# Two AdaLN steps per pass of the first branch, input sums in other attention units, border loads and stores reordered, in a one-core decoder layer

## The chip, the cores and the metric

The kernel runs on one core of one Trainium2 chip. The metric is device time in microseconds (us), the median of several executions. Beside the times there is one profiled execution, recorded by the hardware profiler; rows of it have the start in us from the beginning of its span, the duration, the engine, the line of the kernel and the operation. Five engines work side by side, each in the order of its own instruction stream: TensorE (PE, with PEld for its weight loads), VectorE (DVE), ScalarE (ACT), GpSimd (POOL) and SyncE (SP), which here only issues DMA transfers. ScalarE and GpSimd can issue transfers too.

## The reference

One decoder layer in float32, 1024 tokens, width 1024. AdaLN turns a condition vector into six vectors of 1024, which scale, shift and gate the two halves of the layer:

```python
c_act = jax.nn.silu(c)
mod = (jnp.einsum('bd,de->be', c_act, w_ada[l]) + b_ada[l])[:, None, :]
shift_m, scale_m, gate_m, shift_f, scale_f, gate_f = jnp.split(mod, 6, axis=-1)
u = x * (1.0 + scale_m) + shift_m
y = mixer(u, positions, w_in[l], sinks[l], w_branch_a[l], w_branch_b[l], w_o[l])
x = layer_norm(DEEPNORM_ALPHA * x + (1.0 + gate_m) * y, ln1_g[l], ln1_b[l])
u = x * (1.0 + scale_f) + shift_f
y = swiglu(u, w_gate_up[l], w_down[l])
x = layer_norm(DEEPNORM_ALPHA * x + (1.0 + gate_f) * y, ln2_g[l], ln2_b[l])
```

The mixer has two attentions beside each other. A is a sliding window with 16 query heads and a sink term. B is dilated attention, 24 heads in three patterns of 8, whose three outputs are combined by a softmax over their log-sum-exp. Each goes through its own output matrix, the two results are weighted with sigmoid gates computed from u, added, and multiplied by `w_o`.

## The kernel before

Every product is made from float32 numbers split in two parts, high and low, each of a type (F32R) that TensorE multiplies in one pass: a product is hi·hi + hi·lo + lo·hi, three matmuls. ScalarE makes the high part, VectorE subtracts to get the low part (`split`; L78 and L79 for the weights of the `Weights` streams, L144 and L145 for those of the `Pairs` streams). The `gate` products of the mixer and the gate_up products are made by a seven-product scheme on halves, whose operands are differences of halves of u; these are called t1 to t4 here ("t sums").

The stages, in order. First projections (from the first us on), then 20 **attention units** (12 of B, 8 of A), each in four parts `i` = 0 to 3. While one unit's scores, probabilities and outputs are computed, a generator (`stream`, moved on by `pump`) runs the projections and rotations of the next units between them: a q projection ends in TensorE's tile `pj`, VectorE multiplies it by the cosine (L548, L549), POOL by the sine and adds (L551, L552), ScalarE and VectorE split the result into `qs` (L565, L566), and TensorE multiplies `kh` and `qs` to scores (L624). `tasks(n, i)` is called once in each part and puts in small work for earlier units: sending statistics, `combine_apply` (L774 and L777, merging B's three patterns), the stores of finished A outputs (`scale_a`), and `input_sums`, which makes the t sums. One call chain of `input_sums` handles a row block k and a column half c in four parts: load x into the tile `cst`, scale and shift by ScalarE (L881), four subtractions by VectorE (L883 to L886), store to `t_d`. Before the change units with n%3==1 take one (k, c) and units with n%3==2 the next, for the first twelve units.

At the end of the attention, the **border** to the next stage: the last A outputs go to DRAM (`oa_d`, `wa_d`) from SyncE's queue, SyncE loads the weight pairs of the first gates (`gw.load`), and the t sums, tile by tile (`load_sum`, L1046), into four buffers `xs`; ScalarE (L1019) and VectorE (L1020) split them. Then the **gate products** (L1030): 42 products of 12 matmuls.

In the gate stage begins `ada_steps` (L978), a generator for the AdaLN vectors m = 2 to 5. For each m it loads eight row blocks of `w_ada` (512 KB, tile `a_raw`, two buffers), and adds each, times its entry of c, into `acc` on VectorE (L987 the first, L989 the others); each `next` issues one load and one sum, of the block before. After the eight sums there is one empty step, and then the sum over partitions: for m = 2 and 5 two float32 matmuls against `ones` (L998) and an addition of the bias, for m = 3 and 4 eight narrow matmuls (L1005). Fourteen `next` calls lie in the gate stage.

Then the **branch stage**: 24 passes (`steps`), eight output blocks `dc` each for three operand sets b = 0, 1, 2. A pass makes two products of four blocks from a weight stream (`ws.take`, `ws.step`) and the split attention outputs `parts` (`o_part`, which loads `o_raw` from `oa_d` and `ob_d`), merges them into `merged` (ScalarE for b = 0, VectorE and POOL for b = 1, 2), and calls `next(ada)` once. In the last branch `split_merged` splits a finished row block for the final product, two passes behind; blocks 6 and 7 follow after the loop, and then what is left of `ada_steps`. Then W_o's products, a first layer norm, gate_up, down, and a second layer norm.

The order of work on each engine is the order in which the Python code emits it; a framework adds the waits between engines and for buffers. DMA transfers from one engine's queue are issued in that order, and a transfer that waits holds up those behind it in its queue.

Of the kernel before, what the change touches and what calls it, by code (L numbers as in the profile page):

```python
# [10 lines left out]
F32 = mybir.dt.float32  # L11
F32R = mybir.dt.float32r
# [6 lines left out]
P = 128  # L19
T = 1024  # L20
# [129 lines left out]
def decoder_layer(ctx: ExitStack, tc: tile.TileContext, I, out, dbg=None):  # L150
# [565 lines left out]
    def send_sums(p):  # L716
        es = sums.pop(("es", p))
        pt = ps_t.tile([P, 4, P], F32, name="pt")
        nc.tensor.transpose(pt[:16, 0, :], es.rearrange("p h b -> p (h b)"), ident)
        sr = att.tile([32, P], F32, name="sr", bufs=2)  # L720
        nc.vector.tensor_copy(sr[:16], pt[:16, 0, :])
        nc.sync.dma_start(wa_d[p].rearrange("h (b q) -> (h b) q", q=P), sr[:16])

    def fetch_bcast(key, src):
        last = key in [(B_PAIRS - 1, g) for g in range(3)]
# [5 lines left out]
    def scale_a(p):  # L731
        o = outs.pop(p)
        nc.vector.tensor_tensor(o, o, sums.pop(p), op=OP.mult)
        nc.sync.dma_start(oa_d[p], o)
        if "oa" in dbg:
            nc.sync.dma_start(dbg["oa"][p], o)

# [103 lines left out]
    def tasks(n, i):  # L841

        last = unit(n - 1)
        if "b" in last and i == 0:
            send_stats(last)
            if last["b"][1] == 2:
                combine_load(last["b"][0])
        parts = (combine_shares, combine_weights, lambda p: fetch_bcast((p, 0), wt_d[p, 0]))
        if "b" in last and last["b"][1] == 2 and i > (last["b"][0] == B_PAIRS - 1):
            parts[i - 1 - (last["b"][0] == B_PAIRS - 1)](last["b"][0])  # L850
        if "a" in last and i == 2:
            send_sums(last["a"])
        if "a" in last and i == 3 and last["a"] < A_PAIRS - 1:
            fetch_bcast(last["a"], wa_d[last["a"]])
        last = unit(n - 2)
        if last.get("b", (0, 0))[1] == 2:
            p = last["b"][0]
            if i:
                combine_apply(p, i - 1)
            if (p < B_PAIRS - 1) <= i < 3:  # L860
                fetch_bcast((p, i), wt_d[p, i])
        if "a" in last and i == 1 and last["a"] < A_PAIRS - 1:
            scale_a(last["a"])
        if n % 3 and n < 12:
            input_sums(*divmod(2 * (n // 3) + n % 3 - 1, 2), i)

    def input_sums(k, c, i):

        cols = slice(c * 256, (c + 1) * 256)
        if i == 0:  # L870
            sums["x"] = buf = att.tile([P, T], F32, name="cst", bufs=1)
            for h in range(2):
                nc.sync.dma_start(buf[:, h * TH:(h + 1) * TH].rearrange("p (t c) -> p t c", t=2),
                                  I["xT"][k + 4 * h].rearrange("p (t c) -> p t c", t=2)[:, :, cols])
            return
        buf = sums["x"]
        r11, r12, r21, r22 = [buf[:, x * 256:(x + 1) * 256] for x in range(4)]
        if i == 1:
            for h in range(2):
                part, mod = buf[:, h * TH:(h + 1) * TH], mods[k + 4 * h]  # L880
                nc.scalar.activation(part, part, AF.Identity, bias=mod[:, 0:1], scale=mod[:, 1:2])  # L881
        elif i == 2:
            nc.vector.tensor_tensor(r11, r12, r11, op=OP.subtract)  # L883
            nc.vector.tensor_tensor(r12, r22, r12, op=OP.subtract)
            nc.vector.tensor_tensor(r22, r22, r11, op=OP.subtract)
            nc.vector.tensor_tensor(r21, r21, r22, op=OP.subtract)  # L886
        else:
            nc.sync.dma_start(t_d[:, k, :, cols].rearrange("s p c -> p s c"), buf.rearrange("p (s c) -> p s c", s=4))
# [11 lines left out]
    for s in range(len(subs) + 2):  # L900
        n, i = divmod(s, 4)
        start = ends[min(n, len(units) - 1)] + LEAD if n < len(units) else total
        stop = ends[n + 1] + LEAD if n + 1 < len(units) else total
        at = lambda x: pump(min(int(start + (stop - start) * (i + x) / 4), total - 1))
        if s < len(subs):
            un, qr = subs[s]
            if qr == 0:
                un["st"] = att.tile([P, 2, 2, NB], F32, name="st", bufs=3)
            scores(un, qr)
        at(0.4)  # L910
        if 1 <= s <= len(subs):
            turn_probs(*subs[s - 1])
        if s < len(subs):
            exponentials(*subs[s])
        at(0.8)
        if s >= 2:
            un, qr = subs[s - 2]
            if qr % 2:
                weigh(un, qr // 2)
                if qr == 3:  # L920
                    outs[un["a"] if "a" in un else un["b"]] = un["o"]
                    if "a" in un:
                        keep_sums(un)
                        if un["a"] == A_PAIRS - 1:
                            nc.sync.dma_start(oa_d[un["a"]], un["o"])
        tasks(n, i)
        at(1.0)
    pump(total)
# [46 lines left out]

    shsc = misc.tile([P, 2, KC], F32, name="shsc")

    def ada_steps():  # L978
        for m in (2, 3, 4, 5):
            acc = mix.tile([P, T], F32, name="acc", bufs=1)  # L980
            raws = {}
            for k in range(KC + 1):
                if k < KC:
                    raws[k] = mix.tile([P, T], F32, name="a_raw", bufs=2)
                    nc.sync.dma_start(raws[k], I["w_ada"][k * P:(k + 1) * P, m * D:(m + 1) * D])
                if k == 1:
                    nc.vector.tensor_scalar(acc, raws[0], c_act[:, 0:1], None, op0=OP.mult)  # L987
                elif k > 1:
                    nc.vector.scalar_tensor_tensor(acc, raws[k - 1], c_act[:, k - 1:k], acc, op0=OP.mult, op1=OP.add)  # L989
                yield  # L990
            yield
            if m in (2, 5):
                gt = (mix if m == 2 else misc).tile([P, T], F32, name=f"gate{m}", bufs=1)
                nc.sync.dma_start(gt, I["b_ada"][:, m * D:(m + 1) * D].to_broadcast([P, D]))
                for t in range(2):
                    s = slice(t * TH, (t + 1) * TH)
                    ps = ps_2.tile([P, TH], F32, name="p2")
                    nc.tensor.matmul(ps, ones, acc[:, s], start=True, stop=True)  # L998
                    nc.vector.tensor_tensor(gt[:, s], ps, gt[:, s], op=OP.add)
                nc.vector.tensor_scalar(gt, gt, 1.0, None, op0=OP.add)  # L1000
                gates[m] = gt
            else:
                ps = ps_2.tile([P, TH], F32, name="p2")
                for k in range(KC):
                    nc.tensor.matmul(ps[:, k:k + 1], acc[:, k * P:(k + 1) * P], ones[:, :1], start=True, stop=True)  # L1005
                nc.vector.tensor_tensor(shsc[:, m - 3], ps[:, :KC], b_pp[:, m * 8:m * 8 + 8], op=OP.add)
                if m == 4:
                    nc.vector.tensor_scalar(shsc[:, 1], shsc[:, 1], 1.0, None, op0=OP.add)
# [29 lines left out]
    operand("t4", bigu)  # L1038

    T_AT = {"t1": 0, "t3": 1, "t4": 2, "t2": 3}  # L1040
    t_todo = [(name, k) for name in ("t2", "t1", "t3", "t4") for k in range(4)]
    t_raw = {}

    def load_sum(name, k):
        t_raw[name, k] = gp.tile([P, TH], F32, name="xs", bufs=4)
        nc.sync.dma_start(t_raw[name, k], t_d[T_AT[name], k])  # L1046

    def next_sums(n):
        for _ in range(n):
            if t_todo:  # L1050
                name, k = t_todo.pop(0)
                split_to(name, k, t_raw.pop((name, k)))
                if len(t_todo) > 3:
                    load_sum(*t_todo[3])

    def piece():
        ws.step()
        gw.ready.append(ws.done[ws.used][:2])
        ws.used += 1

    gw.load(0)
    for x in t_todo[:4]:
        load_sum(*x)
    gw.load(1)
    for step in range(4):
        gw.add(0, step)
    acc, gated = {}, {}
# [34 lines left out]
    for n in range(2 * EARLY_PAIRS):  # L1102
# [3 lines left out]
        while len(gw.ready) < min(3, 2 * EARLY_PAIRS - 1 - n):  # L1106
            piece()
        prepare(n + 4 - 2 * EARLY_PAIRS)
        next_sums(2)
        after()  # L1110
        if n in (4, 6, 7):
            early_gate((4, 6, 7).index(n))
# [29 lines left out]
    for p in range(len(gate_pairs)):  # L1142
        ps = dict(zip("ab", acc[p])) if p in acc else {}
        g, last = {}, p == len(gate_pairs) - 1
        for i in range(7):
# [6 lines left out]
            product(gw, ps[bank], i, i in (0, 1, 3))  # L1152
            n += 1
            gate_pair(p, i, ps[bank], ps, g)
            next_sums(2)
            after()
            if (p, i) == (0, 4):
                early_gate(3)
# [48 lines left out]
    for i, (b, dc) in enumerate(steps):  # L1207
# [20 lines left out]
            parts, following = following, []  # L1228
        for t in range(2):
            merge(b, dc, t, ps[t], gts.get(i))  # L1230
        next(ada, None)
        fetch_gate(i + 1)
        if i == 2 * KC + 1:
            mg, _ = wide("m", bigu)
        if i >= 2 * KC + 2:
            split_merged((i - 2 * KC - 2,))
    split_merged(range(6, 8))
    for _ in ada:
        pass
    B.clear()  # L1240
# [238 lines left out]
    for p in range(NF):  # L1479
# [11 lines left out]
        for i in range(7):  # L1491
# [11 lines left out]
            if i in (0, 2):  # L1503
                g[i // 2] = gated.get(p) if i == 0 else None
                if not g[i // 2]:
                    g[i // 2] = kept("g")
                    nc.scalar.activation(g[i // 2], x, AF.Copy)
            if (p, i) == (0, 2):
                late_rest("t4")
            if i in (3, 4):  # L1510
                s[i] = kept(f"c{i}")
# [155 lines left out]
```

## Time and profile before

| What | us |
|---|---|
| Median of three runs | 1835.81 (1834.82 to 1838.19) |
| Profiled execution | 1837.64 |
| Its span, first to last instruction | 1835.9 |
| TensorE busy | 1794.7 (98%) |
| VectorE busy | 1144.2 (62%) |
| ScalarE busy | 811.2 (44%) |
| POOL busy | 619.3 (34%) |
| Mean granted TensorE clock | 0.991 |

The profile gives for each engine its busy time, for each group of instructions what ended the idle time ahead of it, and for stretches of time the busy time of each engine, the granted TensorE clock as a share of full speed, the mean busy share of the 16 DMA engines and the rate in GB/s. A row of a timeline ends with the idle time ahead of it in brackets, and what ended it, where there was any. "x4" counts instructions in a row. Rows of `SPq` are transfers that SyncE issues; their duration is that of the issue. Matmul rows overlap: a new one of 128 × 512 starts about every 0.23 us though each is shown with some 0.4.

### The profile page before, as it was taken

The numbers are of one execution on the slowest core, as the hardware profiler recorded it, in microseconds if no ns is written. First come the engines' busy times: TensorE is split into PE (matmuls) and PEld (weight loads), VectorE is DVE, ScalarE is ACT, GpSimd is POOL, SyncE is SP. The second block draws the span as 40 slices with busy tenths as digits, with TensorE's granted clock in tenths as the row PEclk, the third lists the DMA queues.
The fourth block names the chain that finished last, engine by engine and source line by source line (L and its number), as shares of the span: only waits on it lengthen the run. The fifth ranks groups of instructions, "written<-read, shape, count | busy, mean of one in ns | idle before, by whom it ended". The sixth has DMA issues, their size and how long they took to land.

```text
span 1835.9 us, 24586 instructions
## 1 busy us (share of the span) xinstructions
PE 1794.7 (98%) x8906; PEld 1472.8 (80%) x8906; DVE 1144.2 (62%) x2056; ACT 811.2 (44%) x1726; POOL 619.3 (34%) x397
## 2 busy tenths in 40 slices
PE   9999999999999999999999879999999999999998
PEld 7888887887887888778888758878888888888886
DVE  7745566556656776558648845765655454764557
ACT  6654454454444777665531212743333333421122
POOL 0232233233332232125205633246654333532223
PEclk9999999999999999999999989999999999999999
DMA  9323233233232232266576524032222222432222
GB/s 357 102 74 91 71 99 99 77 93 104 71 95 80 77 101 73 84 233 239 180 224 229 201 92 144 12 124 94 81 92 80 81 86 92 150 129 89 88 80 92
DMA packets 93209, 213.83 MB, mean 116 GB/s; under 512 B 15200, under 2 KB 24992, under 8 KB 93088
## 3 DMA queue, kind: packets, MB, share of 16 engines
q1 hardware_dynamic: 92800, 211.67, 35.1%
q8 instruction: 70, 1.15, 0.3%
q10 hardware_dynamic: 288, 0.59, 0.1%
q14 instruction: 51, 0.42, 0.1%
HBM read 163.62 MB, written 34.96 MB: 108 GB/s over the span
## 4 chain that ended last, share of the span: by engine, by line
PE 85%; DVE 7%; ACT 3%; issue 2%; DMA 2%; POOL 1%; SPq 0%; DVEq 0%; POOLq 0%
PE pf L1030 22%; PE pj L191 8%; PE pj L193 8%; PE pj L192 8%; PE pf L191 5%; PE pf L193 5%; PE pf L192 5%; PE p L1030 4%; PE s L624 4%; PE p L191 3%; PE p L193 3%; PE p L192 3%; PE pt L662 2%; PE po L685 2%; DVE qs L566 1%
## 5 line engine op out<-in xcount | busy, mean ns | idle before, releaser
L191 PE MATMUL pj<-u,w_hi 128*128 128x512 f32 x736 | 304.1, 413 | 0.0
L193 PE MATMUL pj<-u,w_lo 128*128 128x512 f32 x736 | 289.8, 394 | 0.0
L192 PE MATMUL pj<-u,w_hi 128*128 128x512 f32 x736 | 289.5, 393 | 0.0
L551 POOL TENSOR_TENSOR rb<-rb,sin_t 128x512 f32<-128x512 f32 x64 | 85.6, 1338 | 525.6 <-DVE rb L549 454.0
L145 DVE TENSOR_TENSOR w_lo<-r,w_hi 128x512 fp32r<-128x512 f32 x128 | 135.1, 1058 | 137.6 <-ACT w_hi L144 137.2
L79 DVE TENSOR_TENSOR w_lo<-w_raw,w_hi 128x512 fp32r<-128x512 f32 x132 | 120.9, 919 | 85.0 <-ACT w_hi L78 84.4
L191 PEld LDWEIGHTS pj<-u,w_hi 128*128 128x128 f32 x736 | 139.2, 189 | 31.9 <-issue 6.5
L193 PEld LDWEIGHTS pj<-u,w_lo 128*128 128x128 f32 x736 | 139.1, 189 | 31.0
L640 ACT ACTIVATE probs<-probs,st 128x128 f32<-128x128 f32 (+1 forms) x320 | 145.6, 461 | 28.8 <-DVE st L629 28.5
L192 PEld LDWEIGHTS pj<-u,w_hi 128*128 128x128 f32 x736 | 139.7, 190 | 22.7
L62 POOL TENSOR_TENSOR w_raw<-w_raw,gate 128x512 f32<-128x512 f32 x60 | 86.5, 1455 | 163.7 <-DMA w_raw<-in_w_down 117.6
L193 PE MATMUL pf<-wd,h 128*128 128x512 f32 x352 | 137.0, 389 | 0.0
L192 PE MATMUL pf<-wd,h 128*128 128x512 f32 x352 | 137.0, 389 | 0.0
L191 PE MATMUL pf<-wd,h 128*128 128x512 f32 x352 | 137.0, 389 | 0.0
L78 ACT ACTIVATE w_hi<-w_raw 128x512 fp32r<-128x512 f32 x132 | 81.8, 622 | 104.5 <-PE p L192 47.3
L1580 DVE SCALAR_TENSOR_TENSOR zt<-zt,pf 128x512 f32<-128x512 f32 x112 | 75.1, 683 | 79.0 <-PE pf L193 79.0
L552 POOL TENSOR_TENSOR r<-ra,rb 128x512 f32<-128x512 f32 x63 | 115.5, 1833 | 4.9
L664 ACT ACTIVATE ptsb<-pt 128x512 f32<-128x512 f32 (+1 forms) x128 | 63.5, 548 | 95.7 <-PE pt L662 95.4
L126 POOL TENSOR_TENSOR s<-r 128x512 f32<-128x512 f32 x27 | 35.6, 1320 | 173.2 <-DVE w_lo L145 98.5
L565 ACT ACTIVATE qs<-r 64x1024 fp32r<-64x1024 f32 x38 | 40.2, 1059 | 106.4 <-POOL r L552 105.9
L624 PE MATMUL s<-kh,qs 128*128 128x256 f32 (+1 forms) x320 | 80.1, 284 | 6.6 <-DVE qs L566 4.9
L566 DVE TENSOR_TENSOR qs<-r,qs 64x1024 fp32r<-64x1024 f32 x38 | 46.4, 1220 | 57.0 <-ACT qs L565 56.3
(371 smaller groups left out, 4447.9 us busy)
## 6 DMA issues: line engine op xcount, KB each, us to landing
w_raw<-in_w_in SPq DMA_DIRECT2D x100, 256.0 KB
r<-in_w_gate_up SPq DMA_DIRECT2D x44, 512.0 KB
a_raw<-in_w_ada SPq DMA_DIRECT2D x32, 512.0 KB
w_raw<-in_w_down SPq DMA_DIRECT2D x44, 256.0 KB
h_raw<-h_d SPq DMA_DIRECT2D x22, 512.0 KB
h_d<-g SPq DMA_DIRECT2D x39, 256.0 KB
wa<-in_w_ada_m SPq DMA_DIRECT2D x16, 512.0 KB
gt<-ga_d SPq DMA_DIRECT2D x16, 512.0 KB
```

The source lines that it names most:

```text
L62: self.nc.gpsimd.tensor_tensor(self.raws[i], self.raws[i], scale(), op=OP.mult)
L78: self.nc.scalar.activation(hi, raw, AF.Copy)
L79: self.nc.vector.tensor_tensor(lo, raw, hi, op=OP.subtract)
L145: self.nc.vector.tensor_tensor(lo, src, hi, op=OP.subtract)
L191: nc.tensor.matmul(ps, w[0], m[0], start=first, stop=False)
L192: nc.tensor.matmul(ps, w[0], m[1], start=False, stop=False)
L193: nc.tensor.matmul(ps, w[1], m[0], start=False, stop=last)
L551: eng.tensor_tensor(b, b, sin_t[:, s], op=OP.mult)
L552: eng.tensor_tensor(residue_half(res, r, t), by_residue(a, r), by_residue(b, r), op=OP.add)
L624: nc.tensor.matmul(pss[h][:, i, lo:], box["q"][h][:, b * P:(b + 1) * P], ks[h][:, (b - 1 + lo) * P:(b + 1) * P], start=i == 0 and n == 0, ...
L640: nc.scalar.activation(pr, pr, AF.Exp, scale=-1.0, bias=st[:, 0, h, b:b + 1], accum_out=st[:, 1, h, b:b + 1])
L1030: nc.tensor.matmul(ps, w[:, c], m[:, k], start=first and k == 0 and n == 0, stop=k == 3 and n == 2, skip_group_check=True)
```

## The change

Six edits, in the order of the diff:

1. `wa_d` of the last A unit, and `oa_d` of the last two, are stored from POOL's queue in place of SyncE's.
2. All `input_sums` of a row block k run in the unit with n%3==2. Column half 0 starts one part earlier, with its load in part 3 of the unit before, and goes on in parts 0, 1, 2; column half 1 runs in parts 0 to 3 in the tile `wb`. The unit with n%3==1 has only the load.
3. The gate sums of m = 2 and 5 are split into a high and a low part and multiplied by ones in F32R, four matmuls of one pass, with one more step between the split and the matmul.
4. The t sums are loaded in pairs of 512 KB (`load_sums`): t2 into the two `o_raw` buffers and t1 into the two `a_raw` buffers ahead of the first weight pair, t3 after it, t4 and the second weight pair after the second product.
5. Each pass of the first branch calls `next(ada)` twice. `split_merged` runs three passes behind, blocks 5 to 7 after the loop.
6. In gate_up `g_prepare(4)` (splits of weights for coming products) is called ahead of the splits of t4.

The diff:

```diff
@@ send_sums, scale_a
-        nc.sync.dma_start(wa_d[p].rearrange("h (b q) -> (h b) q", q=P), sr[:16])
+        (nc.gpsimd if p == A_PAIRS - 1 else nc.sync).dma_start(wa_d[p].rearrange("h (b q) -> (h b) q", q=P), sr[:16])
...
-        nc.sync.dma_start(oa_d[p], o)
+        (nc.gpsimd if p == A_PAIRS - 2 else nc.sync).dma_start(oa_d[p], o)
@@ tasks, input_sums
-        if n % 3 and n < 12:
-            input_sums(*divmod(2 * (n // 3) + n % 3 - 1, 2), i)
+        if n < 12 and (n % 3 == 2 or n % 3 == 1 and i == 3):
+            k = n // 3
+            for c, step in ((0, (i + 1) % 4), (1, i)) if n % 3 == 2 else ((0, 0),):
+                if n % 3 == 1 or c or i < 3:
+                    input_sums(k, c, step)
...
-            sums["x"] = buf = att.tile([P, T], F32, name="cst", bufs=1)
+            sums["x", c] = buf = att.tile([P, T], F32, name=("cst", "wb")[c], bufs=1)
...
@@ the loop over the units
-                            nc.sync.dma_start(oa_d[un["a"]], un["o"])
+                            nc.gpsimd.dma_start(oa_d[un["a"]], un["o"])
@@ ada_steps
+    ones_r = mix.tile([P, P], F32R, name="ones_r", bufs=1)
+    nc.vector.tensor_copy(ones_r, ones)
...
+                hl = [mix.tile([P, T], F32R, name="a_hl", tag="a_raw", bufs=2) for _ in range(2)]
+                split(*hl, acc)
+                yield
                 for t in range(2):
                     s = slice(t * TH, (t + 1) * TH)
                     ps = ps_2.tile([P, TH], F32, name="p2")
-                    nc.tensor.matmul(ps, ones, acc[:, s], start=True, stop=True)
+                    for x in range(2):
+                        nc.tensor.matmul(ps, ones_r, hl[x][:, s], start=x == 0, stop=x == 1)
@@ the t sums
-    t_todo = [(name, k) for name in ("t2", "t1", "t3", "t4") for k in range(4)]
-    t_raw = {}
-
-    def load_sum(name, k):
-        t_raw[name, k] = gp.tile([P, TH], F32, name="xs", bufs=4)
-        nc.sync.dma_start(t_raw[name, k], t_d[T_AT[name], k])
+    t_todo = [(name, k) for name in ("t2", "t1", "t3", "t4") for k in (0, 2)]
+    t_raw = []
+
+    def load_sums(pool, tag, n):
+        for _ in range(n):
+            name, k = t_todo.pop(0)
+            raw = pool.tile([P, 2, TH], F32, name="xs", tag=tag, bufs=2)
+            nc.sync.dma_start(raw, t_d[T_AT[name], k:k + 2].rearrange("k p c -> p k c"))
+            t_raw.append((name, slice(k, k + 2), raw))

     def next_sums(n):
         for _ in range(n):
-            if t_todo:
-                name, k = t_todo.pop(0)
-                split_to(name, k, t_raw.pop((name, k)))
-                if len(t_todo) > 3:
-                    load_sum(*t_todo[3])
+            if t_raw:
+                split_to(*t_raw.pop(0))
...
+    load_sums(mix, "o_raw", 2)
+    load_sums(mix, "a_raw", 2)
     gw.load(0)
-    for x in t_todo[:4]:
-        load_sum(*x)
-    gw.load(1)
+    load_sums(gp, "xs", 2)
...
-        next_sums(2)
+        next_sums(1)
+        if n == 1:
+            load_sums(mix, "o_raw", 2)
+            gw.load(1)
...
-            next_sums(2)
@@ the branch loop
-        next(ada, None)
+        for _ in range(2 if b == 0 else 1):
+            next(ada, None)
...
-        if i >= 2 * KC + 2:
-            split_merged((i - 2 * KC - 2,))
-    split_merged(range(6, 8))
+        if i >= 2 * KC + 3:
+            split_merged((i - 2 * KC - 3,))
+    split_merged(range(5, 8))
@@ gate_up
             if (p, i) == (0, 2):
+                g_prepare(4)
                 late_rest("t4")
```

More of the change, by code (lines that the diff above doesn't have):

```diff
@@ L875, in input_sums @@
             return
-        buf = sums["x"]
+        buf = sums["x", c]
         r11, r12, r21, r22 = [buf[:, x * 256:(x + 1) * 256] for x in range(4)]
```

## The prediction

> **What bounds the kernel now.** I read the page first, then TensorE's waits, then the timelines of the four places that the change touches. From the page, busy time by engine, the granted clock in 40 slices, and the chain of work that ended last:
>
> ```profile
> PE 1794.7 (98%) x8906; PEld 1472.8 (80%) x8906; DVE 1144.2 (62%) x2056; ACT 811.2 (44%) x1726; POOL 619.3 (34%) x397
> ...
> PEclk9999999999999999999999989999999999999999
> ...
> PE 85%; DVE 7%; ACT 3%; issue 2%; DMA 2%; POOL 1%; SPq 0%; DVEq 0%; POOLq 0%
> ```
>
> TensorE sets the end nearly everywhere, so only its idle time, its half-clock stretches and its own matmuls can be won or lost. Its waits (tile and line, who released it, us in all, times, longest):
>
> ```profile
> PE p L998 <- DVE acc L989: 18.7, 1, 18.7
> PE s L624 <- DVE qs L566: 4.9, 4, 1.5
> PE p L1030 <- DVE w_lo L79: 2.1, 1, 2.1
> ...
> PE p L1030 <- ACT gt L1125: 1.7, 1, 1.7
> ...
> PE pf L1030 <- DVE w_lo L145: 0.8, 1, 0.8
> ```
>
> The first is the AdaLN remainder after the branch loop, the second the attention units, the third and fourth the border between attention and gate products, the last one product of gate_up.
>
> **Part 1: the AdaLN remainder leaves the end of the branch stage.** TensorE, then VectorE, then SyncE's queue there:
>
> ```profile
> 1049.50 0.39 PE L192 MATMUL p<-o_hl,w_hi 128*128 128x512 f32 x1
> 1049.73 0.39 PE L193 MATMUL p<-o_hl,w_lo 128*128 128x512 f32 x1
> 1068.80 3.78 PE L998 MATMUL p<-acc,ones 128*128 128x512 f32 x4 [18.68 <-DVE acc L989]
> 1071.59 1.34 PE L191 MATMUL p<-w_hi,m 128*128 128x512 f32 x1
> 1072.77 0.40 PE L192 MATMUL p<-w_lo,m 128*128 128x512 f32 x1
> ```
> ```profile
> 1057.78 1.90 DVE L989 SCALAR_TENSOR_TENSOR acc<-a_raw,c_act,acc 128x1024 f32<-128x1024 f32 x1
> 1059.60 7.95 DVE L170 TENSOR_TENSOR m<-zt,m 128x512 fp32r<-128x512 f32 x6
> 1067.47 1.27 DVE L989 SCALAR_TENSOR_TENSOR acc<-a_raw,c_act,acc 128x1024 f32<-128x1024 f32 x1
> ```
> ```profile
> 1057.11 0.38 SPq L985 DMA_DIRECT2D a_raw<-in_w_ada  x1
> ```
>
> One step per loop pass leaves m=5's last sum for after the loop, behind the splits, and W_o behind m=5's gate matmul. Two steps in each of the eight first-branch passes bring that matmul into pass 20 of 24. Without it W_o's second matmul would follow the last branch matmul by two pitches of 0.227 us (1049.50 to 1049.73): 1049.73 + 2×0.227 = 1050.19, against 1072.77. That is **−22.6**. VectorE's splits of the last merged rows then limit W_o next; pass 23's follow its merge within about 4 us while W_o's first products use earlier rows, so I put 0 to +1 on it and take 0. m=5's four single-pass gate matmuls now stand in the loop: 4×0.227 = **+0.9**. m=2's gate matmul changes likewise:
>
> ```profile
> 881.30 1.88 PE L998 MATMUL p<-acc,ones 128*128 128x512 f32 x4
> ```
>
> It gets cheaper by about 0.4 (882.61, the next start, less 881.30 is 1.31, against 0.91), but its split on ScalarE and VectorE is only one product ahead and can be up to 1.1 late: −0.4 to +1.1, taken as 0.
>
> **Part 2: two steps per pass in the first branch, the new cost.** TensorE's m=3 sum, VectorE's sums and SyncE's loads as they run now, and the 44 us around them by windows (last columns: granted clock, DMA share, GB/s):
>
> ```profile
> 953.78 1.84 PE L1005 MATMUL p<-ones,acc 128*128 128x1 f32 x16
> ```
> ```profile
> 929.76 1.28 DVE L989 SCALAR_TENSOR_TENSOR acc<-a_raw,c_act,acc 128x1024 f32<-128x1024 f32 x1 [6.19 <-DMA a_raw<-in_w_ada]
> ...
> 933.64 1.28 DVE L989 SCALAR_TENSOR_TENSOR acc<-a_raw,c_act,acc 128x1024 f32<-128x1024 f32 x1 [0.86 <-DMA a_raw<-in_w_ada]
> ...
> 938.00 1.29 DVE L989 SCALAR_TENSOR_TENSOR acc<-a_raw,c_act,acc 128x1024 f32<-128x1024 f32 x1 [1.34 <-DMA a_raw<-in_w_ada]
> ...
> 943.95 1.29 DVE L989 SCALAR_TENSOR_TENSOR acc<-a_raw,c_act,acc 128x1024 f32<-128x1024 f32 x1 [2.92 <-DMA a_raw<-in_w_ada]
> ```
> ```profile
> 921.91 0.98 SPq L985 DMA_DIRECT2D a_raw<-in_w_ada  x1
> ...
> 924.79 0.55 SPq L985 DMA_DIRECT2D a_raw<-in_w_ada  x1
> ...
> 933.25 0.35 SPq L985 DMA_DIRECT2D a_raw<-in_w_ada  x1
> ...
> 936.69 0.33 SPq L953 DMA_DIRECT2D o_raw<-oa_d  x1
> 937.11 0.38 SPq L985 DMA_DIRECT2D a_raw<-in_w_ada  x1
> ```
> ```profile
> 919.00:963.00 44.00, 44.00 (x204) 36.70 (x203) 18.82 (x22) 17.62 (x28) 0.00 (x0) 1.00 0.72 232
> ```
>
> A pass is 24 matmuls of 0.227, 5.44 us; m=3's sum closes pass 6 (seven passes), so the stage begins at T = 953.78 − 7×5.44 = 915.7. From the end of issue to the sum these four loads took 6.9, 8.3, 4.4 and 6.4 us. There are two buffers, so with two sums a pass, sum k needs the load issued after sum k−2: one load time per pass is in series. By the new order m=3's sums 3, 5, 7 form the chain. Load 3 goes out where 921.91 is now and sum 3 runs where 929.76 is, so it ends at 929.76 + 1.28 − 915.7 = T+15.3. Load 5 follows at about T+17 (SyncE is in order and holds it behind a weight load that waits for a split on VectorE). I take 5.4 for a load, the mean of the last two, which have an o_raw load ahead of them as in the new order: it lands at T+22.4, sum 5 ends at T+23.7. Then VectorE splits a weight and an o_part (2.4 with ScalarE's half), load 7 goes out at T+26.2, and lands at T+31.6: sum 7 is done at T+33. Its matmul is due after pass 3, at T + 4×5.44 = 21.8. **TensorE waits about 11** (7 at a load of 3.4, 17 at 8.3; 2 us per us of load), and runs at half clock for 3.4 us after it, as in part 3, +1.4 at this stage's matmul density. m=4's sums have four such passes, 33 to 64, and its matmul is now due at about T+68: +1 (0 to 8; above a load of 6.5 it costs 4 more per us). The third branch's operand splits, later on VectorE, +0.5. Sum **+13.9**, from 7 to 27. Bandwidth itself should not be short: the eight passes move 13 a_raw and four o_raw loads of 512 KB, eight weights of 256 KB and a 512 KB broadcast, 11.5 MB in 44 us or 262 GB/s instead of 232, where a window of part 4 shows 396.
>
> **Part 3: input sums out of the units that rotate late.** VectorE and TensorE in one such unit, and windows with the clock:
>
> ```profile
> 283.67 2.05 DVE L777 TENSOR_TENSOR o<-o 128x1024 f32<-128x1024 f32 x1
> 285.62 0.43 DVE L883 TENSOR_TENSOR cst<-cst 128x256 f32<-128x256 f32 x1
> ...
> 287.34 0.68 DVE L548 TENSOR_TENSOR ra<-pj,cos_t 128x512 f32<-128x512 f32 x1
> ```
> ```profile
> 297.90:301.30 3.40, 3.40 (x9) 2.67 (x9) 3.37 (x2) 0.68 (x2) 3.32 (x2) 0.50 0.00 0
> ...
> 564.12:567.53 3.41, 3.41 (x10) 2.74 (x10) 3.38 (x3) 1.37 (x4) 2.66 (x2) 0.50 0.01 5
> ```
>
> The four subtractions from L883 hold the rotation L548, whose q projection (pj) was complete, from 285.62 to 287.34: 1.72 us. The rotation's chain runs on over POOL (L551, L552) and ends in qs L566, where TensorE stalls by at most 1.5, so moving the subtractions away takes all of it: **−4.9** over the four stalls of the waits. The worst is 0: the units n%3==2 already do the other column half with the same operations at i=2 and stall nobody, but would now do four subtractions at i=1 and four at i=2, each 1.72, with a weight split or a probability scaling queued behind them; an equal stall there would give it all back. Twice the stall is followed by 3.4 us at clock 0.50, as the two windows show; at half rate these hold half the work, −1.7 each, **−3.4** (0 if the clock falls for another reason). The moved operations lie under TensorE's 98%. The Trainium skill ("TensorE: Matmul & The Clock Gate", What's actually happening) has the clock drop only after an idle window of about 3.4 us. The row above shows it at 0.50 after 1.5 us of waiting, so the trace does not agree; by the page this part is worth 4.9 only, and that is rival (d).
>
> **Part 4: the border.** ScalarE and VectorE wait for the t sums; SyncE's queue; POOL; the window with the highest rate:
>
> ```profile
> 802.47 1.32 ACT L1019 ACTIVATE t2h<-xs 128x512 fp32r<-128x512 f32 x2 [6.50 <-DMA xs<-t_d]
> ```
> ```profile
> 794.11 0.33 SPq L734 DMA_DIRECT2D oa_d<-o  x1
> ...
> 797.04 2.15 SPq L1046 DMA_DIRECT2D xs<-t_d  x4
> ```
> ```profile
> 801.96 1.29 POOL L126 TENSOR_TENSOR s<-r 128x512 f32<-128x512 f32 x1 [50.95 <-DMA r<-in_w_in]
> ```
> ```profile
> 804.00:808.00 4.00, 1.82 (x7) 0.95 (x6) 4.00 (x3) 1.35 (x3) 4.00 (x3) 1.00 1.02 396
> ```
>
> ScalarE stands until 802.47 for the first t sum, issued at 797.04 behind the stores and w_in pairs. As pairs in buffers of their own, and with the stores on POOL's queue, the loads can go out some 5 to 8 us earlier; the queued weight split then frees the 2.1 and the 1.7 of the waits above, and two small ones: **−4.5**, from −6 to 0. The price of a store issued by POOL has no row: the nearest are 0.33 on SyncE and, for any operation of POOL's, 1.29. POOL stood idle for 51 us here, so the issue itself hides; a late store is felt only by the o_raw loads of the branch stage, 100 us on, and by tiles that reuse its source. I take 0, and +1 (three times 0.33) as the worst; SyncE has the same 1 us less to do, and the remaining loads in its queue stand that much earlier. The Trainium skill ("DMA: Bandwidth & Descriptors", Issuing engines are not separate DMA queues) says that another issuing engine saves only sequencer time, which would leave about 1 us of this part; no row here has POOL issuing. The last wait of the list, in gate_up:
>
> ```profile
> 1199.69 0.50 PE L1030 MATMUL pf<-b22h,w_lo 128*128 128x512 f32 x1 [0.80 <-DVE w_lo L145]
> ```
>
> Its w_lo is queued on VectorE behind four t4 splits; with g_prepare(4) ahead of them it comes first: **−0.9** (the 0.8 and a pipeline refill of 0.1), and 0 where t4's own splits, now later by two weight splits, are asked for just as soon.
>
> **Sum:** −22.6 + 0.9 + 0 − 4.9 − 3.4 − 4.5 − 0.9 + 13.9 = −21.5. It is made in the profiled execution, 1837.64 with a span of 1835.9; the median of the runs is 1835.81, 1.83 below it, and 1835.81 − 21.5 = **1814**.
>
> **Rivals.**
> (a) The first branch waits less: load 3 and the two after it take 4 us, nearer the 4.4 row than the 8.3. Sum 7 ends 3 + 2×1.4 earlier, the wait is about 5: 1807. For it: nothing else heavy is in the queue after 924.79. Against: three of four rows are over 6.
> (b) The loads are all like the 8.3: wait 17, m=4 another 8, half clock twice: 27, so 1827. For it: the same queue carries 13% more bytes.
> (c) The border pays only the issue time, about 1: 1818; or the four stalls stay: 1823. For it: the t loads stay behind what else SyncE holds (its stores wait for VectorE); against it, the 6.50 wait has a DMA as its releaser.
> (d) No half clock is won, 1818.
> (e) Slower: the first branch's chain of load, sum, load outlasts everything. It decides from a cost of 22.6 − 0.9 + 8.3 + 4.5 + 0.9 = 35.4. From 27 at 8.3 us per load, 6 us more per us of load, that is 9.7 us per load; at 10.5 it gives 1840. Against it: no load of the four took that.
>
> **How the numbers follow.** Forecast 0.50, own range 1809 to 1821; (a) 0.15, (b) 0.14, (c) 0.09, (d) 0.06, (e) 0.06. Range 1803 to 1829: below lies a first branch at its cheapest with all else won, above (e) and part of (b). Within 0.2% (3.7 us, about what a measurement of this kernel can tell from no change) needs a first-branch cost of 32 to 39, the lower part of (e) and the end of (b): 0.04; slower 0.06; faster 0.90.
>
> **What would show it.** Right: no wait of L998 after the loop and W_o's first matmul about 0.5 us after the last branch matmul; a wait of L1005 near 11 us by VectorE's acc, a_raw loads of 4 to 7 us ahead of it; no L624 wait by qs over 0.3 in the four units and no clock 0.50 there; ScalarE's t2h before 798. Wrong: L1005 waiting under 4 or over 20; W_o waiting for m; the border's waits under other names; half clock that follows no stall.

## The result and the profile after

| | before | changed |
|---|---|---|
| Median, us | 1835.81 (1834.78 to 1838.19, five runs) | 1818.42 (1817.84 to 1820.77, five runs) |
| Ratio to before | 1 | 0.9908, 95% interval 0.9894 to 0.9923 |
| Span of the profiled execution, us | 1835.9 | 1819.0 |
| Attention: start to the first gate product | 793.2 | 785.6 |
| Border and gate products | 122.5 | 120.9 |
| Branch stage | 155.9 | 149.6 |
| W_o and first norm, to the first gate_up product | 92.4 | 92.7 |
| The rest | 671.9 | 670.3 |

The stages are counted between the first matmuls of each in the two profiled executions. The kernel became 17.4 us faster by the medians, 16.9 by the spans; 1814 was predicted, with a range from 1803 to 1829. Of all executions behind this document one, of the kernel e11 below, took 4632 us and is left out of its ratio.

In the changed kernel the lines have new numbers: the narrow AdaLN sums L1005 are L1015, the gate sums L998 are L1008, the sums L987/L989 are L993/L995, the gate products L1030 are L1040, the t splits L1019/L1020 are L1029/L1030, the merge L1196 is L1208. TensorE's waits after the change:

```profile
PE p L1015 <- DVE acc L995: 11.2, 1, 11.2
PE p L1040 <- DVE w_lo L79: 2.9, 2, 2.0
PE s L624 <- DVE st L629: 1.7, 6, 0.3
PE p L1008 <- DVE a_hl L170: 1.4, 1, 1.4
PE po L317 <- DVE ones L166: 1.1, 1, 1.1
PE p L191 <- DVE gy L1208: 1.0, 1, 1.0
PE s L624 <- DVE qs L566: 0.6, 1, 0.6
```

The wait of 18.7 at the end of the branch stage is gone, the waits for `qs` fell from 4.9 to 0.6, and a new wait of 11.2 stands in the first branch. At the end of the branch stage W_o's products now follow the last pass (first row) without a wait; their one wait near the start, of 1.0, comes 5 us later, for a bank, a piece of TensorE's output memory that the last merge still reads:

```profile
1055.84 0.39 PE L193 MATMUL p<-o_hl,w_lo 128*128 128x512 f32 x1
1056.07 0.39 PE L191 MATMUL p<-w_hi,m 128*128 128x512 f32 x1
1056.29 0.39 PE L192 MATMUL p<-w_lo,m 128*128 128x512 f32 x1
...
1061.27 0.50 PE L191 MATMUL p<-w_hi,m 128*128 128x512 f32 x1 [0.96 <-DVE gy L1208]
```

TensorE at the new wait, then VectorE's sums 3, 5 and 7 of m=3, SyncE's loads, and windows around the wait (columns: length, then busy time and instructions of PE, PEld, DVE, ACT and POOL, then granted clock, DMA share, GB/s):

```profile
939.60 3.54 PE L1015 MATMUL p<-ones,acc 128*128 128x1 f32 x16 [11.21 <-DVE acc L995]
943.00 0.78 PE L191 MATMUL p<-o_hl,w_hi 128*128 128x512 f32 x1
```
```profile
922.51 1.28 DVE L995 SCALAR_TENSOR_TENSOR acc<-a_raw,c_act,acc 128x1024 f32<-128x1024 f32 x1 [10.55 <-DMA a_raw<-in_w_ada]
...
929.13 1.28 DVE L995 SCALAR_TENSOR_TENSOR acc<-a_raw,c_act,acc 128x1024 f32<-128x1024 f32 x1 [3.54 <-DMA a_raw<-in_w_ada]
...
938.17 1.28 DVE L995 SCALAR_TENSOR_TENSOR acc<-a_raw,c_act,acc 128x1024 f32<-128x1024 f32 x1 [4.82 <-DMA a_raw<-in_w_ada]
```
```profile
913.04 1.32 SPq L991 DMA_DIRECT2D a_raw<-in_w_ada  x2
...
924.86 1.09 SPq L991 DMA_DIRECT2D a_raw<-in_w_ada  x2
...
932.56 0.42 SPq L991 DMA_DIRECT2D a_raw<-in_w_ada  x1
```
```profile
928.39:932.23 3.84, 0.00 (x0) 0.00 (x0) 3.10 (x4) 1.11 (x2) 0.00 (x0) 1.00 0.35 108
932.23:939.60 7.37, 0.00 (x1) 0.03 (x1) 2.55 (x3) 1.06 (x1) 0.00 (x0) 0.50 0.52 175
939.60:945.88 6.28, 6.28 (x23) 5.70 (x24) 3.50 (x5) 0.00 (x0) 0.00 (x0) 0.50 0.69 222
945.88:951.00 5.12, 5.12 (x24) 4.23 (x23) 0.75 (x1) 1.50 (x3) 0.00 (x0) 1.00 0.86 294
```

The reader sees the chain: load, sum, next load out (924.86 after sum 3, 932.56 after sum 5), sum, and each of the three odd sums waits for its own load (bracket: DMA). The DMA engines are half idle meanwhile (0.35 to 0.52): the time of single loads adds up in series, while the sum of all transfers leaves room. TensorE's clock fell during the wait and stayed at half for 6.28 us after its end, in which the narrow sums took 3.4 us (943.00 less 939.60) in place of 1.7.

VectorE in the attention unit that the prediction showed, now without the four subtractions between the two operations:

```profile
283.84 2.04 DVE L777 TENSOR_TENSOR o<-o 128x1024 f32<-128x1024 f32 x1
285.80 0.68 DVE L548 TENSOR_TENSOR ra<-pj,cos_t 128x512 f32<-128x512 f32 x1
```

The border: SyncE's queue, ScalarE, and the stores that POOL issues.

```profile
779.31 2.07 SPq L1058 DMA_DIRECT2D xs<-t_d  x4
781.48 4.02 SPq L112 DMA_DIRECT2D r<-in_w_in  x2
785.59 9.49 SPq L1058 DMA_DIRECT2D xs<-t_d  x2
795.17 4.34 SPq L55 DMA_DIRECT2D w_raw<-in_w_in  x3
```
```profile
794.71 1.06 ACT L1029 ACTIVATE t2h<-xs 128x1024 fp32r<-128x1024 f32 x1 [6.39 <-DMA ga_d<-r]
```
```profile
784.82 0.73 POOL L928 DMA_DIRECT2D oa_d<-o  x1 [41.45 <-ACT o L687]
786.77 0.54 POOL L734 DMA_DIRECT2D oa_d<-o  x1 [1.21 <-DVE ones_r L982]
787.29 0.50 POOL L722 DMA_DIRECT2D wa_d<-sr  x1
```

The t2 loads go out 18 us earlier than before (779 against 797), but the first split starts only 7.8 us earlier, at 794.71: it now waits for the store of `ga_d`, whose source `r` lies in the memory that `t2h` takes over.

### The profile page after: what moved, and what is told of

Its sections match the earlier page's. It is cut to its first block, busy times and chain, and to the rows that moved or that the text cites. A ratio compares the mean times of both kernels' runs of the same rounds, so it can differ in the third digit from the quotient of the medians.

```text
span 1819.0 us, 24567 instructions
## 1 busy us (share of the span) xinstructions
PE 1790.4 (98%) x8906; PEld 1473.9 (81%) x8906; DVE 1139.6 (63%) x2051; ACT 809.9 (45%) x1720; POOL 621.5 (34%) x400
## 4 chain that ended last, share of the span: by engine, by line
PE 87%; DVE 5%; DMA 3%; ACT 2%; issue 1%; POOL 1%; SPq 0%; DVEq 0%; POOLq 0%; ACTq 0%
PE pf L1040 23%; PE pj L191 9%; PE pj L193 8%; PE pj L192 8%; PE pf L191 5%; PE pf L192 5%; PE pf L193 5%; PE p L1040 5%; PE s L624 4%; PE po L685 3%; PE pt L662 3%; PE p L191 2%; PE p L193 2%; PE p L192 2%; DMA a_raw<-in_w_ada 1%
## 5 line engine op out<-in xcount | busy, mean ns | idle before, releaser
L624 PE MATMUL s<-kl,qs 128*128 128x256 f32 (+1 forms) x320 | 80.1, 280 | 0.0
```

What stands on the lines that cost most here:

```text
L624: nc.tensor.matmul(pss[h][:, i, lo:], box["q"][h][:, b * P:(b + 1) * P], ks[h][:, (b - 1 + lo) * P:(b + 1) * P], start=i == 0 and n == 0, ...
```

## The experiments

Four groups of kernels, each beside the kernel before on its own chip (its medians there lay between 1836.2 and 1837.7); times are compared by the ratio to it.

**e1: input sums where they were.**

```diff
-        if n < 12 and (n % 3 == 2 or n % 3 == 1 and i == 3):
...
+        if n % 3 and n < 12:
+            input_sums(*divmod(2 * (n // 3) + n % 3 - 1, 2), i)
...
```

> The changed kernel with the input sums back in the units n%3==1 and n%3==2, all else as changed. Theory: the four waits of L624 for qs (4.9 us in all before, 0.6 after) come back with two stretches of 3.4 us at clock 0.50, so the attention takes 7.8 us more and the whole about 1826. Rival: the half clock there has nothing to do with these waits; then only 4.3 us come back (about 1822.7) and no stretch at 0.50 lies behind a wait for qs.

Ratio 0.9931 (0.9913 to 0.9949), about 4 us slower than the changed kernel where 7.8 were expected; the two intervals overlap. In the profiled execution, with 1830.7 us the longest of its four (the others took 1824.2 to 1824.8), the first gate product came at 791.6, 6.1 later than in the changed kernel's. A wait row, and the only stretch at half clock behind such a wait:

```profile
PE s L624 <- DVE qs L566: 4.6, 3, 1.5
```
```profile
562.52:565.93 3.41, 3.41 (x10) 2.73 (x10) 3.38 (x3) 1.42 (x4) 2.62 (x2) 0.50 0.03 10
```

The waits came back in full, three of 1.5, so the input sums in these units were their cause. The half clock came back behind one of them, where it had stood behind two: this part of the gain is not the same in each profiled execution. The rest of this execution's excess is in the branch stage: m=4's sum, which waited for nothing in the changed kernel, waited 2.6 us here, with 6.8 us at half clock behind it.

**e2: the three border stores on SyncE's queue** (the diff shows one of them).

```diff
-        (nc.gpsimd if p == A_PAIRS - 2 else nc.sync).dma_start(oa_d[p], o)
+        nc.sync.dma_start(oa_d[p], o)
...
```

> The changed kernel with the three border stores (oa_d twice, wa_d) on SyncE's queue again. Theory: the first t2h split waits for the store of ga_d, which lands at 794.7 in any case, so the queue of the other stores is worth little: within 1 us of the changed kernel (1818 to 1819.5). Rival: SyncE's loads of the t sums stand behind stores that wait for VectorE until 786, so the border loses its 3 us again, about 1821.5.

Ratio 0.9926 (0.9912 to 0.9941), some 3 us slower than the changed kernel, with intervals that overlap; border and gate products took 126.7 us in place of 120.9 in the profiled executions. By that stage my theory fell. TensorE's new wait, SyncE's queue and ScalarE in this kernel:

```profile
PE p L1040 <- ACT w_hi L78: 5.3, 1, 5.3
```
```profile
784.25 0.33 SPq L928 DMA_DIRECT2D oa_d<-o  x1
...
787.05 3.50 SPq L1058 DMA_DIRECT2D xs<-t_d  x4
```
```profile
792.68 1.06 ACT L1029 ACTIVATE t2h<-xs 128x1024 fp32r<-128x1024 f32 x1 [4.61 <-DMA xs<-t_d]
...
803.78 0.63 ACT L78 ACTIVATE w_hi<-w_raw 128x512 fp32r<-128x512 f32 x1 [8.56 <-DMA w_raw<-in_w_in]
```

The loads stand behind three stores that wait for their data, and start at 787.05, 7.7 us later. The t2 split does not suffer, it is even earlier, so the `ga_d` store does not land at 794.7 in any case, as the theory had it; the weights at the end of the train of loads do: ScalarE gets them at 803.78 where the changed kernel has them at 800.25, and TensorE waits 5.3 and then runs 6.8 us at half clock. So the rival's mechanism is right and its price was too low.

**e3: the extra steps spread over the branch loop.**

```diff
-        for _ in range(2 if b == 0 else 1):
+        for _ in range(2 if i in (3, 6, 8, 10, 12, 14, 18, 19) else 1):
             next(ada, None)
```

> The changed kernel with its eight extra AdaLN steps no longer in the eight first-branch passes but one each in passes 3, 6, 8, 10, 12, 14, 18 and 19, so that m=5's gate matmul stands in pass 20 as it does now. Theory (the wait of L1015 comes from the loads in series when two sums share a pass): L1015 waits under 1 us, no half clock in the branch stage, 11.2 + 3.3 = 14.5 us less, about 1804. Rival (the loads are slow in this stage for any order, or W_o's start is bound by something else): L1015 or L1008 waits elsewhere, gain under 7, above 1811.

Ratio 0.9847 (0.9832 to 0.9861), 0.6% less than the changed kernel, with intervals apart. No wait of L1015 is left and no half clock behind it; the branch stage takes 135.4 us in place of 149.6, the 14.2 that theory put at 14.5. W_o gives 2.7 of it back:

```profile
PE p L191 <- DVE gy L1208: 2.5, 1, 2.5
```
```profile
1049.24:1052.65 3.41, 2.96 (x7) 2.38 (x8) 3.41 (x4) 0.63 (x1) 2.93 (x3) 0.50 0.80 261
```

**e4: the AdaLN edits alone, on the kernel before** (edits 3 and 5 of the change).

> The kernel before with the AdaLN edits alone (two steps per first-branch pass, the split gate sums, split_merged one pass later). Theory, by the terms measured in the changed kernel: tail -22.6, m=5's matmuls +0.9, m=2's gate +1.35, first branch +14.5, a wait of W_o for its bank +1.1: -4.75, about 1831. Rival: the parts lean on each other (the border's loads and the AdaLN loads share SyncE's queue and buffers), and AdaLN alone gives more than 8 or nothing.

Ratio 0.9960 (0.9944 to 0.9976), 7 us less than before. Branch stage and W_o together 240.9 in place of 248.3. That is 2.5 us more than the 4.75 of the theory; TensorE waited 8.7 for the m=3 sum here in place of 11.2, which accounts for the difference.

**e5: half the bytes per m=3 load**, each read twice by its sum. The kernel leaves out the second half of m=3's vector.

```diff
-                    nc.sync.dma_start(raws[k], I["w_ada"][k * P:(k + 1) * P, m * D:(m + 1) * D])
+                    n = D // 2 if m == 3 else D
+                    nc.sync.dma_start(raws[k][:, :n], I["w_ada"][k * P:(k + 1) * P, m * D:m * D + n])
...
```

> The changed kernel with m=3's a_raw loads cut to their first 512 columns (256 KB in place of 512), which the sums on VectorE read twice; so the second half of m=3's vector is not computed. Every sum, matmul and wait stays. L1015 waited 11.2 in the changed kernel and 8.7 to 9.6 in three other kernels with two steps per pass. Theory (load times in series, three of them ahead of the last sum): about 1 us less for each of the three, a wait of 5.5 to 8. Rival (the order of SyncE's and VectorE's work sets it, the size of the loads does not): 8.7 to 11.2 as it is.

```profile
PE p L1019 <- DVE acc L999: 6.9, 1, 6.9
```

One run. The wait is as the theory of loads in series has it, against 8.5 to 11.2 in the five kernels with whole loads and two steps per pass.

**e7: tile names reordered, t3 loads later.**

```diff
-    for name in ("t2", "t1", "t3"):
+    for name in ("t1", "t3", "t2"):
         operand(name, low)
...
-    load_sums(gp, "xs", 2)
+        if n == 0:
+            load_sums(gp, "xs", 2)
```

> The changed kernel with two edits at the border: the operand tiles are taken in the order t1, t3, t2, so that t2h no longer lies where the tile r is still being stored to ga_d, and the two t3 loads are issued after the first product. Theory: ScalarE's first t2h runs before 792 (794.7 in the changed kernel) and the w_raw loads go out by 788 in place of 795, so the two waits of L1040 for w_lo (2.9) fall under 0.5; from the first gate product to the branch stage 118 us in place of 120.9. Rival: the bandwidth of all the loads together sets it; the waits stay above 2.

1818.0 in one run, border and gate products 121.2; the waits for w_lo were 2.6, and the first split still stood behind the store:

```profile
794.51 1.06 ACT L1029 ACTIVATE t2h<-xs 128x1024 fp32r<-128x1024 f32 x1 [6.60 <-DMA ga_d<-r]
```

Reordering the names left t2h in the place it had: the edit did not do what it was for, and the later t3 loads alone are worth nothing that this run can tell.

**e8 and e9: the edits of e3 and e7 together, with the split of the gate sums one step earlier (the lines shown); e9 also with the last weight step behind the last merge.**

```diff
-            yield
-            if m in (2, 5):
+            if m not in (2, 5):
+                yield
+            if m in (2, 5):
...
                 split(*hl, acc)
                 yield
+                yield
...
```

> The changed kernel with the spread of e3, the two border edits of e7, and the split of the gate sums one step earlier (an empty step behind it). Theory: terms add up. Spread -10.5 as e3 had it, border -2.9, the wait of L1008 for a_hl -1.5: 15 less than the changed kernel, with a ratio to before of 0.983. Rival: what is saved ahead of W_o only lengthens its wait for the bank of the last merge (1.0 in the changed kernel, 2.5 in e3): ratio above 0.986.

> As e8, with the last weight step of the branch loop emitted behind the merge of the last pass in place of ahead of it. Theory: the merge (gy L1208) no longer stands behind that step's weight split on VectorE, W_o's wait for its bank falls from 2.5 to about 1.3 and the stretch at clock 0.50 behind it goes, 2 to 3 us less than e8. Rival: the weight split is what W_o needs first; then W_o waits for w_lo instead and the time is that of e8.

Ratios 0.9856 (0.9839 to 0.9873) and 0.9845 (0.9830 to 0.9860): both as e3, and not the 0.983 that the theory of e8 asked for. In e8 the wait for m=2's split (L1008 in the changed kernel) is gone, and border and gate products take 119.9 us where e3 takes 121.4. But the branch stage is 2.2 us longer than in e3 (137.6 against 135.4): there TensorE waits 0.4 for m=4's sum, with 3.4 us at half clock behind it (rows in the last section). W_o waits 2.0 in e8 and 2.7 in e9, so moving the one weight step was no cure.

**e10 and e11: m=5 finished two passes earlier**, with two of the steps (first lines) in the last gate pair; **e11 also with t2's operands where t4's were** and with the late t3 loads of e7. Both have the split step of e8.

```diff
+                if i < 2:
+                    next(ada, None)
...
+        for _ in range(2 if i in (2, 4, 6, 8, 11, 12, 14, 16) else 1):
...
```

and in e11 also

```diff
-    for name in ("t2", "t1", "t3"):
+    for name in ("t4", "t1", "t3"):
         operand(name, low)
-    operand("t4", bigu)
+    operand("t2", bigu)
...
```

> The changed kernel with the gate split one step earlier (as e8), two more AdaLN steps in the first two products of the last gate pair, and the other extra steps one each in branch passes 2, 4, 6, 8, 11, 12, 14 and 16, so that m=5's gate matmul stands in pass 18 instead of 20. Theory: VectorE runs about one pass behind at the end of the branch stage in e3, e8 and e9 because m=5's last sums and gate operations come so late; with them two passes earlier W_o's wait for gy (2.0 to 2.7 there) falls under 1 and L1015 waits under 0.5: 2 to 3 less than e8's 1811, about 1808. Rival: the splits of the merged rows and the weight scaling set VectorE's lag alone; W_o still waits 2 or more, the time is e8's.

> As e10, with t2's operand tiles where t4's were and t4's in the other pool, so that t2h does not share memory with the tile r of the last ga_d store (in e7 the order of the names alone had left it there), and with the t3 loads issued after the first product. Theory: ScalarE's first t2h starts before 791 (794 in e7, e8 and e9, behind ga_d), the two waits of L1040 for w_lo (2.1 to 2.9 in all) go: 2.5 to 4 less than e10. Rival: t2h then waits for its own loads, which share the DMA engines with everything else there (some 400 GB/s from 787 to 797), and the border keeps 2 us of waits.

Ratios 0.9874 (0.9859 to 0.9889) and 0.9859 (0.9839 to 0.9879). W_o's wait is gone as theory had it, and another takes its place at the start of the third branch (e10):

```profile
PE p L192 <- DVE o_hl L170: 4.5, 1, 4.5
```

The border did what was expected of it: in e11 ScalarE's first t2h starts without any wait, TensorE's waits for w_lo in the border fall from 2.6 to 0.3, and border and gate products take 118.5 us against 121.3 in e10.

```profile
788.16 1.05 ACT L1031 ACTIVATE t2h<-xs 128x1024 fp32r<-128x1024 f32 x1
```

**e12 and e13: e11 with the extra steps in passes 2, 4, 5, 6, 8, 11, 16, and without pass 5.**

> As e11, with the extra AdaLN steps in branch passes 2, 4, 5, 6, 8, 11 and 16 (in e11 2, 4, 6, 8, 11, 12, 14, 16), m=5's gate matmul in pass 19. Theory: the new wait of L192 for o_hl in e10 and e11 (4.5 and 4.6, with 3.4 to 6.8 us at clock 0.50 behind it) came from the pairs of sums in passes 12 and 14, whose second load VectorE awaits ahead of the last o_part splits; without them it falls under 0.5 and 6 us go: a ratio to before of 0.982 to 0.983, about 1805. Rival: the o_parts are late because their loads share the queue with the gates' loads; the wait stays at 4.

> As e12 without the pair in pass 5, so that every AdaLN step from there on comes a pass later at most and m=5's gate matmul stands in pass 20, as in e3 and e8. Theory (W_o's wait depends on how late m=5 ends on VectorE): 0 in e10 and e11 (pass 18), 2 to 2.7 in e3, e8 and e9 (pass 20): here about 2 and 2 us more than e12. Rival: two sums in one pass late in the loop were the cause, not the pass of the matmul; then W_o's wait is under 1 here too and both have one time.

Ratios 0.9854 (0.9836 to 0.9872) and 0.9849 (0.9835 to 0.9864). The first row is of e12, the second of e13:

```profile
PE p L1017 <- DVE acc L995: 3.2, 1, 3.2
```
```profile
PE p L191 <- DVE gy L1213: 4.1, 1, 4.1
```

The wait for o_hl is gone in e12, as expected, and 1.3 in e13; the time of e12 stayed at e11's, where 6 us less were expected. In its place came a wait for m=4's sum, whose steps now come a pass earlier, in e12, and W_o's, twice what was expected, in e13. Among e3 and e8 to e13 W_o's wait goes with the pass of m=5's gate matmul: 0 at pass 18, 0.5 at 19, 2.0 to 4.1 at 20. That the pass is its cause is not shown. In the kernels with two steps in each pass of the first branch this matmul stands in pass 20 too, and W_o waits 0 to 1.0: wherever W_o waits little, TensorE has waited 3 us or more earlier in the branch stage, which would also give VectorE time to catch up.

Branch stage and W_o together take 242.3 us in the changed kernel, 230.8 in e3, and 231.4, 232.7, 233.4, 233.0, 234.2 and 234.5 in e8 to e13. Where one wait was taken away another grew: for the bank of W_o, for o_hl, for m=4's sum. No version was measurably faster than e3. All seven, e3 and e8 to e13, lie clearly below both kernels; the lowest, e3, e9 and e13 (0.9847, 0.9845, 0.9849), by about 0.6% of the time against the changed one. e3's steps with e11's border were not tried together.

## Why the prediction was right

By its terms, each against the two profiled executions:

| Term | Predicted | Measured |
|---|---|---|
| Tail of the branch stage | −22.6 | −22.6 (no wait of L998; W_o follows the last pass) |
| W_o's bank behind it | 0 (0 to 1) | +1.1 |
| m=5's gate matmul in the loop | +0.9 | +0.9 |
| m=2's gate sum | 0 (−0.4 to 1.1) | +1.35 |
| First branch: wait for m=3's sum | +11 | +11.2 |
| Half clock behind it | +1.4 | +3.3 |
| m=4's sum, and the third branch's splits | +1.5 | 0 |
| Attention | −8.3 | −7.6 |
| Border | −4.5 | −3.0 |
| t4 in gate_up | −0.9 | −1.5 |
| Sum | −21.5 | −16.9, as the spans differ |

The tail, the units and the first branch went by the mechanisms that the prediction named. Its chain of load 3, sum 3, load 5, sum 5, load 7, sum 7 is what the rows show, and e3 and e5 confirm it by spreading the steps and by halving the loads. That the wait came out at 11 is partly luck: in the profiled executions of e7, e4, e1 and e2, with the same order, it was 8.5, 8.7, 8.8 and 9.6. Two of its inputs were off in opposite directions: load 3 took 8.6 us from the end of its own issue and not 6.9, and loads 5 and 7, at 3.9 and 5.2, were quicker than 5.4. Of the signs that the prediction named, one failed besides: a wait of 0.6 for qs was left in one unit, where it had been 0.2.

The 4.6 us between forecast and measurement by the spans (4.1 by the medians) are made of sizes:

- The **clock** term. The prediction let half clock last 3.4 us behind the wait. It lasted 6.28 (the third window row above), and the narrow sums that open this stretch ran at half speed too. Measured: 1.7 for them and 1.6 for the products after them. The +1.4 was too low by its own row as well: TensorE is busy for all 44.00 us of that window, and 3.4 us at half clock then cost 1.7, as in part 3.
- The **border**. The loads did go out earlier than assumed, and the wait of 1.7 for gt went; the waits for w_lo, which the prediction counted as won, are 2.9 where they were 2.1. What was late next was not a load but the `ga_d` store under t2h, which no step of the prediction named; e11 shows that 2.8 us were left there. All that was won hangs on the stores' move, which the prediction costed as SyncE's own issue time and a place in the queue: without it (e2) the stage is 5.7 us longer, and longer than before the change.
- **m=2's gate sum**: the four matmuls came to 2.66 us, because TensorE stood 1.4 for VectorE's split in their midst. This is beyond the bound of 1.1 that one product of lead was given; e8, with a step more in between, has no such wait.
- **W_o's bank** came out at the upper end of its bound; VectorE runs some 4.5 us behind at the last pass.
- **m=4's sum** cost nothing in this execution. In e1's it waited 2.6 us, so a price for it was in place.
- The **attention** came within 0.7 of its term, but 0.8 of the 7.6 is another wait's: the one for u in the first 20 us, which lies between 0.3 and 1.2 in all these kernels, happened to be 1.1 before and 0.3 after.

Of the rivals, (a) and (b) were the same chain with other load times, and the measured case lies between. (c) and (d) gave 1818, the number that was measured, but not by what happened: against (c), the border gave 3.0 and not 1, and the three stalls of 1.5 went; against (d), both stretches at half clock in the attention went, though what makes the clock fall is half open, as the last section tells. Rival (e) needed loads near 10 us; only load 3 came close. The Trainium skill's rule on issuing engines ("DMA: Bandwidth & Descriptors", Issuing engines are not separate DMA queues), by which the stores' move saves sequencer time alone, about 1 us by the prediction's estimate, does not cover this case: in e2 the queue was held up by stores that waited for their data, and 5.7 us went with it.

## What to carry to other kernels

When work is moved from an end where it is waited for into a loop with room, ask for each buffer pair how many loads lie in series in one pass, not only whether engines and bandwidth have time: one step per pass hides a load of 4 to 8 us, two steps with two buffers put one into every pass. A transfer that waits for its data holds up the whole queue behind it (7.7 us in e2), so stores of just finished results go to a queue that has no urgent loads. And when an early load does not make its user earlier, look at what else lives in the user's output memory.

## What was not expected of the hardware

The stretches at half clock begin and end on a fixed grid of 3.41 us in each execution: the two in the prediction's windows begin 564.12 − 297.90 = 266.22 us apart, 78 times 3.413, and the one behind L1015 lasts 13.65 = 4 × 3.413, as it did in e1, e2, e4 and e7 with waits of 8.5 to 9.6. So a shorter wait need not shorten it; behind e5's wait of 6.9 it lasted 10.24, three times 3.413. The Trainium skill ("TensorE: Matmul & The Clock Gate", What's actually happening) tells of a free-running window of this length, and the trace agrees. By its rule the clock falls after an idle window; here it also fell after windows that were busy for half, and not always. Windows of before (two pairs) and of e4, each with a wait of 1.5 for qs and the window behind it:

```profile
294.48:297.89 3.41, 1.87 (x12) 1.63 (x12) 3.35 (x6) 3.36 (x12) 0.00 (x1) 1.00 0.23 77
297.90:301.30 3.40, 3.40 (x9) 2.67 (x9) 3.37 (x2) 0.68 (x2) 3.32 (x2) 0.50 0.00 0
427.60:431.01 3.41, 1.88 (x10) 1.29 (x8) 3.22 (x4) 3.34 (x9) 0.00 (x0) 1.00 0.07 25
431.01:434.42 3.41, 3.41 (x18) 2.92 (x19) 3.38 (x5) 2.04 (x8) 2.06 (x1) 1.00 0.15 55
```
```profile
426.62:430.03 3.41, 1.87 (x11) 1.30 (x10) 3.32 (x4) 3.33 (x9) 0.00 (x0) 1.00 0.13 36
430.03:433.44 3.41, 3.41 (x12) 2.83 (x12) 3.38 (x5) 1.77 (x6) 2.27 (x2) 0.50 0.11 43
```

With the same busy time (1.87 and 1.88) the clock fell once and stayed once. Over the nine such waits in before, e1 and e4 it fell in the four that began 0.5 to 1.5 us into a window of the grid and stayed in the five that began 1.8 us or later. Why the place matters is open. It fell once with hardly a wait: in e8 a window that held the sixteen narrow sums of m=4 and a wait of 0.4 was followed by one at 0.50.

```profile
976.82:980.23 3.41, 3.04 (x22) 2.48 (x21) 3.41 (x4) 1.58 (x2) 2.18 (x2) 1.00 0.68 261
980.23:983.64 3.41, 3.41 (x10) 2.64 (x9) 3.38 (x5) 0.00 (x0) 2.95 (x2) 0.50 0.83 286
```

So the attention part gains 1.5 us per removed wait, and 1.7 more for those that begin early in a window of the grid.
